# Two-layer hybrid decoder trunk: x normalised before its split, gates leaving PSUM by ScalarE, memory projection first in a layer

## The chip, the cores and the metric

The kernel runs on one core of a Trainium2 chip. The metric is the device time of one execution in microseconds. A core has five engines that run side by side and wait for each other through semaphores: TensorE (PE in the profile, with its weight loads as PEld), VectorE (DVE), ScalarE (ACT), GpSimd (POOL) and SyncE (SP), which here issues the transfers.

## What is computed

Two layers over 1024 tokens of width 1024. Each layer normalises x, projects it by one wide matrix into the inputs of four branches and their gates, runs the branches, and merges them:

```python
h = rms_norm(x, norm_g)
z = h @ w_in          # a_u a_v a_gate b_cq b_ckv b_krope b_gate c_in c_gate m_q m_gate merge_logits
y_a = chunked_spatial_gating(gelu(a_u), gelu(a_v), ...) * silu(a_gate)
y_b = latent_attention(b_cq, b_ckv, b_krope, ...) * silu(b_gate)
y_c = s5_layer(c_in, ...) * silu(c_gate)
y_m = memory_attention(m_q, rms_norm(mem, m_norm_g), ...) * silu(m_gate)
gates = sigmoid(merge_logits + b_merge)
x = x + sum(gates[i] * (y_i @ w_br_i)) @ w_out
```

All of it is float32. TensorE gets each operand as two fp32r parts, hi and lo = value - hi, and forms a product from three matmuls (hi by hi, hi by lo, lo by hi).

## The kernel before, in words

**Tiles.** x is kept transposed: eight chunks of 128 features by 1024 tokens. `make_xg` (L367) multiplies a chunk by `norm_g`, writes its hi part by ACT and its lo part by DVE, and squares it for the norm; the squares are summed over the chunks on GpSimd in `xacc`. The row norm `rs` (one number for each token) is not applied there. Since tokens run along the columns of every product with x, a block of the projection (128 output features by 1024 tokens) can be multiplied by the row norm when it leaves PSUM: `rsb` is the norm of all tokens, copied to every partition, and DVE multiplies each block by it. `x_stats` forms `rs` from `xacc` (16 column sums by TensorE, then a chain of small DVE operations for the inverse square root), and `x_rows` forms `rsb` by four fp32r matmuls.

**A block.** `cm` loads 128 output features' weights (512 KB), splits them (DVE the hi part, mostly GpSimd the lo part, `wsplit` L146), and `block_into` (L184) issues 48 matmuls of 128x128 by 128x512 into a PSUM tile of 1024 columns. There are two such tiles (`pmm`), two smaller for transposes and sums (`ptr`), and two of 512 columns for background work (`pbg`; one in the attention part).

**Order of a layer** (`run`). S5 input (two blocks, `s5_input`), norm, the two blocks of the latent keys and values (`latents`, called ckv below), then the smaller stages of rotary key, memory query, S5 scan (`s5_scan`), keys and values, memory keys and values (`mem_kv`), memory attention, the query latents; in the second part the attention sweep, branch A, the merges (`merge`) and the output projection, whose blocks also prepare the next layer's x. The Tile framework orders each engine's instructions from this program and from priorities. `background` (L1224) is called for 10 of the 32 merge gates and 6 other gate blocks of a layer; their matmuls have the lowest priority and stand wherever TensorE would otherwise wait. Each half (512 tokens) goes to its own `pbg` tile:

```python
for h in range(2):
    with low():
        ps = self.pbg.tile([P, 512], F32, tag="bg", ...)
        self.half_block(ps, (hi, lo), self.xg, hs)
    self.tt(x[:, hs], ps, self.rsb[:, hs], MUL)
```

so the matmuls have the low priority and the multiplication on the way out has the usual one.

**The start.** After the constants, SP loads one S5 input weight, x chunk 0, the second weight and the other chunks. `mem_kv` loads the two raw tiles of the memory itself, splits them, squares them for the memory norm, and projects them with 48 matmuls (four chunks of weights, `m_w_kv`) in the middle of the layer.

Of the kernel before, what the change touches and what calls it, by code (L numbers as in the profile page):

```python
# [8 lines left out]
F32 = mybir.dt.float32  # L9
F32R = mybir.dt.float32r  # L10
# [34 lines left out]
class Trunk:  # L45
    def __init__(self, ctx, tc, a, out, depth):
# [12 lines left out]
        self.nid = 0  # L59
# [86 lines left out]
    def wsplit(self, ap, n, gains=None, keep=False, bg=False, raw=None, eng=None):  # L146

        raw = (self.wraw(bg) if raw is None else raw)[:, :n]
        self.nc.sync.dma_start(out=raw, in_=ap)
# [260 lines left out]
    def x_stats(self):  # L410
        self.rs = self.keep(self.inv_rms(self.tok_sums(self.xacc), 8, D), 8, "rs")

    def x_rows(self):

        hi, lo = self.U("dgh", F32R), self.U("dgl", F32R)
        v = lambda x: x.rearrange("p (t j) -> p t j", t=8)
        wide = lambda x: x.unsqueeze(2).to_broadcast([P, 8, P])
        ident = self.ident.unsqueeze(1).to_broadcast([P, 8, P])
        rh = self.ss(8, "rsh").bitcast(F32R)
        rl = self.ss(8, "rsl")  # L420
        nc = self.nc
        nc.vector.tensor_copy(rh, self.rs)
        self.tt(rl, self.rs, rh.bitcast(F32), SUB)
        self.tt(v(hi), ident, wide(rh.bitcast(F32)), MUL)
        self.tt(v(lo), ident, wide(rl), MUL)
        ps = self.mm()
# [125 lines left out]
    def s5_input(self, l):  # L552

        w = self.wcin if l == 0 else [self.wsplit(self.a["w_cm"][l, B_CIN + b], 1024) for b in range(2)]
# [4 lines left out]
        res = []  # L559
# [87 lines left out]
    def mem_kv(self, l):  # L647
        nc, a = self.nc, self.a
        mh, ml, msum = [], [], []
        mrd = self.U("mrd")  # L650
        for h in range(2):
            raw = self.U("mraw")
            nc.sync.dma_start(out=raw, in_=a["memT"][h])
            hi, lo = self.U("mh", F32R), self.U("ml", F32R)
            self.split(hi, lo, raw)
            sq = self.U("msq")
            self.act(sq, raw, AF.Square)
            rd = mrd[:, h * 256:(h + 1) * 256]
            nc.vector.reduce_sum(out=rd, in_=sq.rearrange("p (b m) -> p m b", b=4), axis=AX.X)
            mh.append(hi)  # L660
            ml.append(lo)
            msum.append(rd)
# [974 lines left out]
```

## Time and profile before

| | |
|---|---|
| median of 3 runs | 2491.41 us (2484.19 to 2493.68) |
| profiled execution | 2490.22 us, its span 2488.5 us |
| mean granted clock of TensorE in it | 0.981 |
| TensorE busy | 2370.0 us, 95% of the span |
| VectorE busy | 1288.2 us, 52% |
| ScalarE busy | 687.4 us, 28% |
| GpSimd busy | 798.1 us, 32% |

The profile is of one execution; the span runs from its first instruction to its last. "Busy" is the time in which an engine had an instruction under way. In a timeline each row is one instruction or a run of alike ones, `out<-in` in the program's names, and in brackets how long the engine had been idle before it and what released it. The granted clock is a share of full speed (2.4 GHz); near 0.5 TensorE is on the lower of its two levels, 1.2 GHz.

### The profile page before, as it was taken

How to read it: one execution, taken by the hardware profiler on the slowest of the kernel's cores; microseconds unless marked ns; L12 is line 12 of the kernel's file. 1: busy time of each engine (PE TensorE's matmuls, PEld its weight loads, DVE VectorE, ACT ScalarE, POOL GpSimd, SP SyncE). 2: the span in 40 equal slices, each digit the busy share in tenths (PEclk: the TensorE clock that was granted, in tenths of full speed). 3: DMA queues.
4: the chain of work that ended last, by engine and by line, in shares of the span. 5: the costliest groups of instructions: out<-in, count | busy, mean ns of one | idle time of the engine just before them, and what ended most of it. 6: DMA issues, size and time to landing. Idle time of an engine off the chain costs nothing. (4 is left out here: it accounts for less than half of the span.)

```text
span 2488.5 us, 28967 instructions
## 1 busy us (share of the span) xinstructions
PE 2370.0 (95%) x11566; PEld 1930.0 (78%) x11566; DVE 1288.2 (52%) x2002; ACT 687.4 (28%) x1110; POOL 798.1 (32%) x616
## 2 busy tenths in 40 slices
PE   7999989989999999999999998999999999999999
PEld 5777677867778887888887876787777788888887
DVE  7554675267776323336335557714688763233351
ACT  3111254136662101111111213622466420011010
POOL 6633112432303214343336431133232132234411
PEclk9989899999999999999999999999999999999999
DMA  3226343242222113123332263413333311112242
GB/s 140 83 75 195 98 148 98 78 126 76 89 70 66 60 34 102 61 92 111 127 95 96 78 186 106 144 45 109 113 90 98 110 50 51 51 60 85 85 166 72
DMA packets 91704, 237.61 MB, mean 95 GB/s; under 512 B 25201, under 2 KB 34353, under 8 KB 91569
## 3 DMA queue, kind: packets, MB, share of 16 engines
q1 hardware_dynamic: 91568, 235.76, 29.7%
q8 instruction: 91, 1.49, 0.3%
q14 instruction: 45, 0.36, 0.0%
HBM read 175.27 MB, written 60.46 MB: 95 GB/s over the span
## 5 line engine op out<-in xcount | busy, mean ns | idle before, releaser
L96 POOL TENSOR_TENSOR wl<-wr,wh 128x1024 fp32r<-128x1024 f32 (+3 forms) x125 | 295.9, 2367 | 998.5 <-DVE wh L152 671.2
L152 DVE CAST wh<-wr 128x1024 fp32r<-128x1024 f32 (+2 forms) x110 | 78.9, 718 | 613.4 <-PE mm L176 542.4
L176 PE MATMUL mm<-xh,wh 128*128 128x512 f32 x1216 | 379.4, 392 | 9.6 <-ACT xh L106 8.3
L176 PE MATMUL mm<-xl,wh 128*128 128x512 f32 x1216 | 376.5, 391 | 0.4 <-DVE xl L103 0.4
L176 PE MATMUL mm<-xh,wl 128*128 128x512 f32 x1216 | 376.1, 390 | 0.2 <-POOL wl L96 0.2
L176 PEld LDWEIGHTS mm<-xh,wh 128*128 128x128 f32 x1216 | 228.0, 189 | 59.5 <-ACT xh L106 8.3
L176 PEld LDWEIGHTS mm<-xl,wh 128*128 128x128 f32 x1216 | 229.3, 189 | 48.8 <-DVE xl L103 0.9
L176 PEld LDWEIGHTS mm<-xh,wl 128*128 128x128 f32 x1216 | 229.1, 188 | 48.4 <-POOL wl L96 0.6
L176 PE MATMUL bg<-xh,bh 128*128 128x512 f32 x576 | 229.8, 416 | 21.6 <-DVE bgx L96 21.6
L176 PE MATMUL bg<-xh,bl 128*128 128x512 f32 x576 | 224.5, 409 | 2.4 <-POOL bl L96 2.4
L176 PE MATMUL bg<-xl,bh 128*128 128x512 f32 x576 | 226.7, 410 | 0.0
L96 POOL TENSOR_TENSOR bl<-br,bh 128x1024 fp32r<-128x1024 f32 x36 | 93.5, 2597 | 305.1 <-DVE bh L152 164.3
L106 ACT ACTIVATE cmn<-cmn,bmh 128x1024 f32<-128x1024 f32 x44 | 50.7, 1151 | 440.0 <-DVE cmn L96 440.0
L176 PE MATMUL pv<-pT,v 128*128 128x256 f32 x640 | 131.4, 307 | 27.3 <-DVE pT L96 21.2
L176 PEld LDWEIGHTS bg<-xh,bh 128*128 128x128 f32 x576 | 111.7, 195 | 48.0 <-DVE bgx L96 28.7
L176 PEld LDWEIGHTS pv<-pT,v 128*128 128x128 f32 x640 | 98.3, 191 | 61.2 <-DVE pT L96 33.1
L96 DVE TENSOR_TENSOR pT<-tr,pT 128x512 fp32r<-128x512 f32 x192 | 129.1, 685 | 30.5 <-ACT pT L106 28.0
L176 PEld LDWEIGHTS bg<-xh,bl 128*128 128x128 f32 x576 | 111.4, 194 | 23.6 <-POOL bl L96 3.2
L106 ACT ACTIVATE pT<-tr 128x512 fp32r<-128x512 f32 x192 | 109.9, 597 | 64.2 <-PE tr L1065 56.0
L176 PEld LDWEIGHTS bg<-xl,bh 128*128 128x128 f32 x576 | 112.1, 195 | 18.6 <-issue 0.2
L1024 DVE TENSOR_REDUCE mx<-mm 128x1 f32<-128x128 f32 (+7 forms) x128 | 96.5, 754 | 36.3 <-PE mm L176 35.6
L106 ACT ACTIVATE pr<-mm,nm,qs 128x128 f32<-128x128 f32 (+7 forms) x128 | 105.9, 832 | 26.3 <-DVE nm L103 26.0
(447 smaller groups left out, 4382.9 us busy)
## 6 DMA issues: line engine op xcount, KB each, us to landing
wr<-in_w_cm_dram SPq DMA_DIRECT2D x76, 512.0 KB, 3.6
br<-in_w_cm_dram SPq DMA_DIRECT2D x36, 512.0 KB, 3.7
bgscr<-bgx SPq DMA_DIRECT2D x20, 512.0 KB, 3.7
gate<-bgscr SPq DMA_DIRECT2D x20, 512.0 KB, 5.4
ysscr<-bgx SPq DMA_DIRECT2D x16, 512.0 KB, 2.6
br<-ysscr SPq DMA_DIRECT2D x16, 512.0 KB, 3.5
wr<-in_w_out_dram SPq DMA_DIRECT2D x16, 512.0 KB, 3.9
bgr<-riscr SPq DMA_DIRECT2D x24, 256.0 KB, 5.4
```

Source lines behind the costliest of these rows:

```text
L96: (eng or self.nc.vector).tensor_tensor(out=out, in0=x, in1=y, op=op)
L106: self.nc.scalar.activation(out, x, f, **k)
L152: self.nc.vector.tensor_copy(hi[:, :n], raw)
L176: self.nc.tensor.matmul(out, lhsT, rhs, start=start, stop=stop)
L1024: nc.vector.reduce_max(out=mx, in_=ps[:, 0:n], axis=AX.X)
```

## The change

- **x is normalised before its split.** `make_xg` now comes after `x_stats`, and multiplies each chunk in place by `norm_g` and `rsb` (eight DVE operations for a layer) before ACT and DVE split it. No block is multiplied by `rsb` on its way out any more. `rsb` comes from two fp32 matmuls in place of four fp32r ones; `x_rows` and `s5_spread` go. The squares (`x_square`) are ACT's, the sums DVE's in layer 0, GpSimd's in layer 1 except the last.
- **Gates leave PSUM by ACT.** The tanh of a gate reads PSUM itself; plain blocks are copied by ACT. In `background` the whole body has the low priority. The S5 input goes straight to `ct` by an ACT copy.
- **Memory first.** `mem_load` and `mem_project` stand at the start of the program for layer 0, and in the output projection of layer 0 (blocks 4 and 7) for layer 1; ACT copies the projection to `mkv`, which `mem_kv`, now right behind ckv, reads. SP loads two memory tiles and two of their weights ahead of x, and no S5 weight early.
- **38 buffers** of 4 KB for each partition in the general pool, 35 before, and a dynamic DMA scratch of 1024.

```diff
 def wsplit(...)
-        self.nc.sync.dma_start(out=raw, in_=ap)
+        if ap is not None:
+            self.nc.sync.dma_start(out=raw, in_=ap)
...
-    def make_xg(self, l, c, xt):
-        hi, lo = self.U(f"xh{c}", F32R), self.U(f"xl{c}", F32R)
-        self.split(hi, lo, xt, gain=self.norm_g[:, l * 8 + c:l * 8 + c + 1])
+    def x_square(self, c, xt, eng):
         if c == 0:
             self.xacc = self.wraw(True)
-            self.xg = []
-            if l == 0:
-                self.tt(self.xacc, xt, xt, MUL, eng=self.nc.gpsimd)
-            else:
-                self.act(self.xacc, xt, AF.Square)
+            self.act(self.xacc, xt, AF.Square)
         else:
             sq = self.U("xsq")
             self.act(sq, xt, AF.Square)
-            self.tt(self.xacc, self.xacc, sq, ADD, eng=self.nc.gpsimd)
-        self.xg.append((hi, lo))
+            self.tt(self.xacc, self.xacc, sq, ADD, eng=eng)
+
+    def make_xg(self, l, xs):
+        self.xg = []
+        for c, xt in enumerate(xs):
+            hi, lo = self.U(f"xh{c}", F32R), self.U(f"xl{c}", F32R)
+            self.stt(xt, xt, self.norm_g[:, l * 8 + c:l * 8 + c + 1], self.rsb, MUL, MUL)
+            self.split(hi, lo, xt)
+            self.xg.append((hi, lo))
...
     def x_stats(self):
-        self.rs = self.keep(self.inv_rms(self.tok_sums(self.xacc), 8, D), 8, "rs")
-    def x_rows(self):
...
-            self.mmr(ps[:, hs], self.onesr, hi[:, hs], True, False)
-            self.mmr(ps[:, hs], self.onesr, lo[:, hs], False, True)
-        self.rsb = self.U("rsb")
-        self.act(self.rsb, ps, AF.Copy)
+        rs = self.inv_rms(self.tok_sums(self.xacc), 8, D)
+        dg = self.U("dg")
+        self.tt(dg.rearrange("p (t j) -> p t j", t=8), self.ident.unsqueeze(1).to_broadcast([P, 8, P]),
+                rs.unsqueeze(2).to_broadcast([P, 8, P]), MUL)
+        self.rsb = self.U("rsb")
+        for h in range(2):
+            hs = slice(h * 512, (h + 1) * 512)
+            ps = self.tr()
+            self.nc.tensor.matmul(ps, self.onesr.bitcast(F32), dg[:, hs], start=True, stop=True)
+            self.act(self.rsb[:, hs], ps, AF.Copy)
...
     def s5_input(self, l):
-        w = self.wcin if l == 0 else [self.wsplit(self.a["w_cm"][l, B_CIN + b], 1024) for b in range(2)]
+        w = [self.wsplit(self.a["w_cm"][l, B_CIN + b], 1024) for b in range(2)]
...
-            cr = self.U("cr")
-            self.act(cr, ps[b], AF.Copy)
-            res.append(cr)
-        return res
-    def s5_spread(self, cin):
-        for b, cr in enumerate(cin):
             ct = self.U("ct")
-            self.tt(ct.rearrange("p (s j) -> p j s", s=8), cr.rearrange("p (j s) -> p j s", s=8),
-                    self.rsb.rearrange("p (j s) -> p j s", s=8), MUL)
+            self.act(ct.rearrange("p (s j) -> p j s", s=8), ps[b].rearrange("p (j s) -> p j s", s=8), AF.Copy)
...
-    def mem_kv(self, l):
+    def mem_load(self, l):
+        raws = [self.U("mraw") for _ in range(2)]
+        for h in range(2):
+            self.nc.sync.dma_start(out=raws[h], in_=self.a["memT"][h])
+        self.mem, mrd = [], self.U("mrd")
...
+    def mem_project(self, l):
+        nc, a = self.nc, self.a
+        mh, ml, msum = [[m[k] for m in self.mem] for k in range(3)]
+        self.rsm = self.keep(self.inv_rms(self.tok_sums(msum[0], 2), 2, D), 2, "rsm")
         ps = self.mm()
...
+        self.mkv = self.U("mkv")
+        self.act(self.mkv, ps, AF.Copy)
+
+    def mem_kv(self, l):
+        nc, rsm = self.nc, self.rsm
+        pv = self.mkv.rearrange("p (t w) -> p t w", t=2)
...
     def cmn(self, l, bi):
         t = self.U("cmn")
-        self.tt(t, self.cm(l, bi, self.xg), self.rsb, MUL)
+        self.act(t, self.cm(l, bi, self.xg), AF.Copy)
...
     def background(...):
         x = ft("bgx")
-        for h in range(2):
-            hs = slice(h * 512, (h + 1) * 512)
-            with low():
+        sg = ft("bgs") if y is not None else x
+        with low():
+            for h in range(2):
+                hs = slice(h * 512, (h + 1) * 512)
                 ps = self.pbg.tile([P, 512], F32, tag="bg", name=self._n("bg"))
                 self.half_block(ps, (hi, lo), self.xg, hs)
-            self.tt(x[:, hs], ps, self.rsb[:, hs], MUL)
-        with low():
+                self.act(sg[:, hs], ps, AF.Tanh, scale=0.5, **({} if bias is None else {"bias": bias}))
+                if y is not None:
+                    self.stt(x[:, hs], sg[:, hs], 1.0, ps, ADD, MUL)
             if y is None:
-                self.act(x, x, AF.Tanh, scale=0.5, bias=bias)
                 nc.sync.dma_start(out=dst, in_=x)
                 return
-            sg = ft("bgs")
-            self.act(sg, x, AF.Tanh, scale=0.5)
-            self.stt(x, sg, 1.0, x, ADD, MUL)
...
     def merge(...):
-                g = self.cmn(l, B_MRG + 8 * i + c)
-                self.act(g, g, AF.Tanh, scale=0.5, bias=self.bm_half[:, l * 32 + 8 * i + c:l * 32 + 8 * i + c + 1])
+                g = self.U("gate")
+                self.act(g, self.cm(l, B_MRG + 8 * i + c, self.xg), AF.Tanh, scale=0.5, bias=self.bm_half[:, l * 32 + 8 * i + c:l * 32 + 8 * i + c + 1])
...
     def run(self):
-        self.wcin = [self.wsplit(a["w_cm"][0, B_CIN], 1024, eng=nc.vector)]
+        self.mwr = [self.wraw() for _ in range(2)]
+        self.mem_load(0)
+        for c in range(2):
+            nc.sync.dma_start(out=self.mwr[c], in_=a["m_w_kv"][0, c])
         xs = [self.U("x") for _ in range(8)]
         for c in range(8):
             nc.sync.dma_start(out=xs[c], in_=a["xT"][c])
...
+        self.setup()
+        self.mem_project(0)
         for c in range(8):
-            self.make_xg(0, c, xs[c])
-        self.setup()
+            self.x_square(c, xs[c], nc.vector)
...
-            cin = self.s5_input(l)
             self.x_stats()
+            self.make_xg(l, xs)
+            self.s5_input(l)
...
-            self.ckv, kacc = self.latents(l, B_CKV, 2, "kv", self.gkv_norm, ((self.x_rows, lambda: self.s5_spread(cin)),))
+            self.ckv, kacc = self.latents(l, B_CKV, 2, "kv", self.gkv_norm)
+            self.mem_kv(l)
...
             scan(1)
-            self.mem_kv(l)
             glu()
...
                 if l < self.L - 1:
-                    self.make_xg(l + 1, c, xr)
+                    if c == 7:
+                        self.mem_project(l + 1)
+                    self.x_square(c, xr, nc.vector if c == 7 else nc.gpsimd)
+                    xs[c] = xr
+                    if c == 4:
+                        self.mwr = []
+                        self.mem_load(l + 1)
...
-NU = 35
+NU = 38
```

Where the instructions stand. **ACT, start of layer 0, after.** `wh` are weights of the memory projection, `mkv` its copy out of PSUM, `br` and `xsq` the squares of x:

```order
L106 ACTIVATE br_282<-x_116 128x1024
L106 ACTIVATE wh_242<-wr_240,consts_90 128x512 x2
L106 ACTIVATE wh_262<-wr_260,consts_90 128x512 x2
L106 ACTIVATE mkv_280<-mm_203 128x1024
L106 ACTIVATE xsq_284<-x_117 128x1024
L106 ACTIVATE xsq_287<-x_118 128x1024
```

Five more squares follow. The copy `mkv` stands between the first square and the other seven. Before, these squares alternate with the hi parts, and no `mkv` is there.

**ACT, end of layer 0's output projection, after.** `xres` are the output blocks, the last being `xres_9338`:

```order
L106 ACTIVATE xsq_9335<-xres_9276 128x1024
L106 ACTIVATE wh_9442<-wr_9440,consts_90 128x512 x2
L106 ACTIVATE wh_9462<-wr_9460,consts_90 128x512 x2
L106 ACTIVATE wh_9482<-wr_9480,consts_90 128x512 x2
L106 ACTIVATE mkv_9500<-mm_9419 128x1024
L106 ACTIVATE xsq_9502<-xres_9338 128x1024
L106 ACTIVATE rsb_9538<-tr_9539 128x512
L106 ACTIVATE rsb_9538<-tr_9542 128x512
L106 ACTIVATE xh_1622_9545<-xres_8885 128x1024
```

Here `mkv` stands ahead of the square of the last block only; the others are through.

**PE, background blocks, before** (layer 0, behind ckv; `bg_614` and `bg_640` are the halves of one block, `bh` and `bl` its weights):

```order
L176 MATMUL bg_640<-xh_20_126,bl_610 128x512
L176 MATMUL bg_614<-xh_23_133,bh_609 128x512
L176 MATMUL bg_640<-xh_23_133,bh_609 128x512
L176 MATMUL bg_614<-xl_24_134,bh_609 128x512
L176 MATMUL bg_640<-xl_24_134,bh_609 128x512
L176 MATMUL bg_614<-xh_23_133,bl_610 128x512
L176 MATMUL bg_640<-xh_23_133,bl_610 128x512
L176 MATMUL bg_614<-xh_26_140,bh_609 128x512
```

**PE, background blocks, after** (layer 0, a later place; `bg_1023` and `bg_1049` are the halves of one block):

```order
L177 MATMUL bg_1023<-xh_79_373,bl_1019 128x512
L177 MATMUL bg_1023<-xh_81_378,bh_1018 128x512
L177 MATMUL bg_1023<-xl_82_379,bh_1018 128x512
L177 MATMUL bg_1023<-xh_81_378,bl_1019 128x512
L177 MATMUL bg_1049<-xh_67_343,bh_1018 128x512
L177 MATMUL bg_1049<-xl_68_344,bh_1018 128x512
L177 MATMUL bg_1049<-xh_67_343,bl_1019 128x512
L177 MATMUL bg_1049<-xh_69_348,bh_1018 128x512
```

The halves took turns before; now the second begins when the first has ended.

## Rows read from the trace of the kernel before

**Rows 1.** The page, busy time of TensorE.

```profile
PE 2370.0 (95%) x11566; PEld 1930.0 (78%) x11566; DVE 1288.2 (52%) x2002; ACT 687.4 (28%) x1110; POOL 798.1 (32%) x616
```

**Rows 2.** PE's waits (total, times, longest): whole run; 60 to 500 us; 1320 to 1640 us.

```profile
PE bg L176 <- DVE bgx L96: 21.6, 15, 3.9
...
PE bg L176 <- DVE bgx L96: 12.5, 7, 3.9
...
PE tr L500 <- DVE stt L96: 5.3, 1, 5.3
PE bg L176 <- DVE bgx L96: 5.1, 4, 2.7
```

**Rows 3.** Windows by stage: length, busy of PE, PEld, DVE, ACT, POOL; clock, DMA, GB/s.

```profile
240.00:300.00 60.00, 50.59 (x214) 38.60 (x213) 37.19 (x73) 8.52 (x11) 9.35 (x5) 0.83 0.35 109
...
1640.00:1720.00 80.00, 80.00 (x353) 64.44 (x352) 22.98 (x22) 15.20 (x15) 30.06 (x14) 1.00 0.25 80
```

**Rows 4.** Narrow windows, the same columns.

```profile
38.00:46.00 8.00, 7.86 (x29) 6.85 (x30) 5.93 (x23) 0.00 (x0) 5.99 (x4) 0.57 0.30 82
...
260.00:281.00 21.00, 21.00 (x62) 15.75 (x61) 7.84 (x14) 2.00 (x2) 0.00 (x0) 0.51 0.18 51
...
1741.00:1752.00 11.00, 7.11 (x18) 5.26 (x19) 10.45 (x29) 2.01 (x2) 4.72 (x2) 0.53 0.67 211
```

**Rows 5.** Timeline of PE, 0 to 75 us: start, us, instruction, idle before and releaser.

```profile
8.27 1.22 PE L176 MATMUL mm<-xh,wh 128*128 128x512 f32 x2 [8.27 <-ACT xh L106]
...
38.15 3.27 PE L388 MATMUL tr<-ones,br 128*128 128x1 f32 x16 [3.99 <-POOL br L96]
...
73.08 0.61 PE L176 MATMUL mm<-xh,wl 128*128 128x512 f32 x2
```

**Rows 6.** Timeline of PE, 258.5 to 259.5 us.

```profile
258.81 0.71 PE L620 MATMUL tr<-sx,cst 64*128 64x127 f32 x4 [2.88 <-DVE sx L96]
259.44 0.50 PE L176 MATMUL bg<-xh,bh 128*128 128x512 f32 x1
```

**Rows 7.** Timeline of DVE, 0 to 10 us.

```profile
5.71 0.69 DVE L152 CAST wh<-wr 128x1024 fp32r<-128x1024 f32 x1 [2.29 <-DMA wr<-in_w_cm_dram]
...
8.27 1.70 DVE L152 CAST wh<-wr 128x1024 fp32r<-128x1024 f32 x1 [0.60 <-DMA wr<-in_w_cm_dram]
```

**Rows 8.** Groups of DVE by form: times, busy us, mean ns; idle before and releasers.

```profile
L96 DVE TENSOR_TENSOR bgx<-bg,rsb 128x512 f32<-128x512 f32 x72 | 47.4, 684 | 43.2 <-PE bg L176 42.9
...
L103 DVE SCALAR_TENSOR_TENSOR xl<-x,consts,xh 128x1024 fp32r<-128x1024 f32 x8 | 20.4, 2623 | 0.0
...
L103 DVE SCALAR_TENSOR_TENSOR wl<-wr,consts,wh 128x512 fp32r<-128x512 f32 x16 | 12.7, 807 | 3.8 <-ACT wh L106 3.8
...
L103 DVE SCALAR_TENSOR_TENSOR xl<-xres,consts,xh 128x1024 fp32r<-128x1024 f32 x8 | 10.4, 1296 | 10.0 <-ACT xh L106 10.0
...
L96 DVE TENSOR_TENSOR ml<-mraw,mh 128x1024 fp32r<-128x1024 f32 x4 | 4.9, 1222 | 1.2 <-ACT mh L106 1.2
```

**Rows 9.** Timeline of ACT, 30 to 36 us.

```profile
32.84 1.03 ACT L106 ACTIVATE cr<-mm 128x1024 f32<-128x1024 f32 x1 [9.08 <-PE mm L176]
```

**Rows 10.** Timeline of DVE, the memory norm, 290 to 294 us.

```profile
290.64 0.16 DVE L100 TENSOR_SCALAR ms<-tr 128x2 f32<-128x2 f32 x1 [0.42 <-PE tr L388]
...
293.66 0.17 DVE L407 COPY rsm<-ry 128x2 f32<-128x2 f32 x1
```

**Rows 11.** Groups of PE by form, 0 to 73.6 us.

```profile
L176 PE MATMUL bg<-xh,bh 128*128 128x512 f32 x4 | 2.0, 512 | 0.0
...
L176 PE MATMUL mm<-dgh,onesr 128*128 128x512 f32 x2 | 1.1, 550 | 3.2 <-DVE s5w L96 3.2
```

**Rows 12.** Line 516, the fp32 matmuls (records: ns min/median/max).

```profile
L516 PE MATMUL tr<-sd,shift x64: 270/275/275, 98.6 to 1417.3; 128*128 128x128 f32 x64
```

**Rows 13.** Groups of ACT by form.

```profile
L106 ACT ACTIVATE pT<-tr 128x512 fp32r<-128x512 f32 x192 | 109.9, 597 | 64.2 <-PE tr L1065 56.0 <-PE tr L1139 6.7
```

**Rows 14.** Timeline of POOL, 15 to 36 us.

```profile
15.86 19.18 POOL L96 TENSOR_TENSOR br<-br,xsq 128x1024 f32<-128x1024 f32 x6
```

More of the change, by code (lines that the diff above doesn't have):

```diff
@@ L58, in __init__ @@
         self.dp = mk(name="dp", bufs=1, space=bass.MemoryType.DRAM)
-        self.nid = 0
+        self.nid, self.ppv = 0, None
     def _n(self, base):
@@ L644, in s5_glu @@
             nc.sync.dma_start(out=self.gscr[b], in_=sg)
-    def mem_kv(self, l):
-        nc, a = self.nc, self.a
-        mh, ml, msum = [], [], []
-        mrd = self.U("mrd")
-        for h in range(2):
[L652 to L662, printed above, removed]
-        self.tt(msum[0], msum[0], msum[1], ADD)
-        rsm = self.keep(self.inv_rms(self.tok_sums(msum[0], 2), 2, D), 2, "rsm")
+    def mem_load(self, l):
[4 more added lines that the diff above has]
+        for h in range(2):
+            hi, lo = self.U("mh", F32R), self.U("ml", F32R)
+            self.split(hi, lo, raws[h])
+            sq = self.U("msq")
+            self.act(sq, raws[h], AF.Square)
+            rd = mrd[:, h * 256:(h + 1) * 256]
+            self.nc.vector.reduce_sum(out=rd, in_=sq.rearrange("p (b m) -> p m b", b=4), axis=AX.X)
+            self.mem.append((hi, lo, rd))
+        self.tt(mrd[:, 0:256], mrd[:, 0:256], mrd[:, 256:512], ADD)
+    def mem_project(self, l):
+        nc, a = self.nc, self.a
+        mh, ml, msum = [[m[k] for m in self.mem] for k in range(3)]
+        self.rsm = self.keep(self.inv_rms(self.tok_sums(msum[0], 2), 2, D), 2, "rsm")
         ps = self.mm()
@@ L667, in mem_kv @@
             gains = [self.gm_norm[:, l * 8 + 2 * c + k:l * 8 + 2 * c + k + 1] for k in range(2)]
-            wh, wl = self.wsplit(a["m_w_kv"][l, c], 1024, gains)
+            wh, wl = self.wsplit(None if c < len(self.mwr) else a["m_w_kv"][l, c], 1024, gains,
+                                 raw=self.mwr[c] if c < len(self.mwr) else None)
             for k in range(2):
@@ L675, in mem_kv @@
                                  wa[:, k * 512:(k + 1) * 512], kt == 0 and j == 0, kt == 7 and j == 2)
-        pv = ps.rearrange("p (t w) -> p t w", t=2)
+        self.mkv = self.U("mkv")
[3 more added lines that the diff above has]
+        pv = self.mkv.rearrange("p (t w) -> p t w", t=2)
         sq = self.U("ksq")
@@ L727, in mq_stage @@
             nc.vector.tensor_copy(ssm.rearrange("p (t h) -> p t h", t=8)[:, :, 2 * p:2 * p + 2], self.head_sums(sqs[p], self.sel2, 2))
-        pre = self.ss(32, "pre")
-        nc.vector.tensor_copy(pre.rearrange("p (t h) -> p t h", t=8), self.rs.unsqueeze(2).to_broadcast([P, 8, 4]))
-        r = self.inv_rms(ssm, 32, 64, pre)
+        r = self.inv_rms(ssm, 32, 64)
         self.mqs = self.lp.tile([P, 32], F32, tag="mqs", name=self._n("mqs"))
@@ L754, in krope @@
         kc, kr = self.U("kc"), self.U("kr")
-        self.tt(kc[0:64, :], ps[0:64, :], self.rsb[0:64, :], MUL)
+        self.act(kc[0:64, :], ps[0:64, :], AF.Copy)
         pt = self.tr()
@@ L804, in rope_query_tables, with latents @@
         return res
-    def latents(self, l, first, n, base, gain, between=()):
+    def latents(self, l, first, n, base, gain):
         res = []
@@ L811, in latents @@
             ps = self.cm(l, first + b, self.xg)
-            if b < len(between):
-                for f in between[b]:
-                    f()
             hi, lo = self.U(f"{base}h{b}", F32R), self.U(f"{base}l{b}", F32R)
@@ L887, in q_stage @@
         pv = pt[:, 0:80].rearrange("p (t m) -> p m t", t=8)
-        alq = self.inv_rms(pv[:, 8], 8, 768, self.rs)
+        alq = self.inv_rms(pv[:, 8], 8, 768)
         pre, ssq = self.ss(64, "pre"), self.ss(64, "ssq")
@@ L1282, in silu2 @@
     def silu2(self, l, bi):
-        x = self.cmn(l, bi)
+        x = self.cm(l, bi, self.xg)
         sg = self.U("sg")
@@ L1319, in branch_a @@
             v, tmp = self.U("av"), self.U("avt")
-            self.tt(v.rearrange("p (t c) -> p t c", t=4), ps.rearrange("p (t c) -> p t c", t=4),
-                    self.rs[:, 4 * tg:4 * tg + 4].unsqueeze(2).to_broadcast([P, 4, 256]), MUL)
+            self.act(v, ps, AF.Copy)
             self.gelu2(v, v, tmp)
@@ L1455, in run @@
             self.mq_stage(l)
-            self.bkv = self.keep(self.inv_rms(self.tok_sums(kacc), 8, 256, self.rs), 8, "bkv")
+            self.bkv = self.keep(self.inv_rms(self.tok_sums(kacc), 8, 256), 8, "bkv")
             def scan(q):
@@ L1625 @@
     arrs = _layout(inputs)
-    nc = bacc.Bacc("TRN2", target_bir_lowering=False, num_devices=1)
+    nc = bacc.Bacc("TRN2", target_bir_lowering=False, num_devices=1, dynamic_dma_scratch_size=1024)
     arrays, aps = {}, {}
```

16 lines of the change are left out of this document (removed).

## The prediction, on record before the changed kernel's time was known

> **What bounds the kernel now.** I read the page's totals first, then PE's waits, the windows by stage, and the timelines of the start. TensorE (PE) is busy for 2370.0 us of the 2488.5 us span [rows 1], so the kernel is long because PE has that much to multiply; only 118 us are idle. The change leaves the count of large matmuls alone. It can gain or lose in two places only: PE's idle gaps, and the stretches after a gap in which the granted clock is low. The largest group of gaps is the background blocks waiting for VectorE (DVE) to empty their PSUM bank, 21.6 us in 15 waits [rows 2]. The stretches show that not every gap matters alike: 1640 to 1720 us is full at clock 1.00, while 240 to 300 us has 50.59 us of work in 60 at a mean clock of 0.83 [rows 3]. Inside the latter PE is never idle from 260 to 281 us, yet it runs at 0.51, the lower of the clock's two levels, behind a gap of 2.88 us at 258.81; 38 to 46 us (0.57) follows one of 3.99 us, and 1741 to 1752 us (0.53) has 3.9 us of idle time in it [rows 4 to 6].
>
> **1. The start of layer 0.** Today PE begins the S5 input blocks at 8.27 us, as soon as one chunk of x has landed, and needs no row norm for that; the norm is applied when results leave PSUM. Its chain runs beside the matmuls and shows as a wait of 3.99 us at 38.15; both ckv blocks are done at 73.5 [rows 5]. After the change nothing that reads x can start before the norm is known. What PE has instead is the memory projection (48 matmuls), which needs weights of its own. Loads follow each other by 1.28 us: between DVE's first and second weight casts, at 5.71 and 8.27, three transfers of 512 KB end, two intervals [rows 7]. On SP's queue now stand two raw memory tiles, two weights, eight chunks of x, then two more weights whose buffers must first come free. The fourth weight is the fourteenth such load and lands at 5.7 + 13 x 1.28 = 22.3. Its hi and lo copies take about 0.8 each by halves [rows 8], and its 12 matmuls 0.45 apiece at the low clock, to which PE falls while it waits for weights: 24.0 + 5.4 = about **30**. Moving x two loads back costs nothing, since its squares are not needed before that.
>
> For ScalarE (ACT) stands in order: the copy mkv, which needs the projection's last matmul, is listed ahead of seven of the eight squares. So the norm's chain begins at 30: mkv and the first square 1.0 each, as the pass `cr` of the same size [rows 9]; seven DVE adds at 1.22, priced by the subtraction ml of equal shape [rows 8], 8.6; 16 column sums 3.3 [rows 5]; the rsqrt chain, 290.64 to 293.83 where the memory norm has it now, 3.2 [rows 10]; the diagonal, a DVE pass of the same size, 1.2; two fp32 matmuls and a copy out; the product with x 1.3, as xl with xres [rows 8], and its hi copy 1.1. The trace has no fp32 matmul of 512 columns. Below, it costs what the fp32r one does, 0.55 [rows 11]; above, the fp32 matmul of 128 columns, two records of 0.275 for each, scales to 2.2 [rows 12]. I take 1.7 each, near the upper end, because the fp32 row is the same number format, and 0.6 for the copy, as for pT, 128x512 out of PSUM [rows 13]: 4.0. Sum: 30 + 1.0 + 9.6 + 3.3 + 3.2 + 1.2 + 4.0 + 2.4 = **54.7**. From there 96 matmuls of the S5 input and 96 of ckv at 0.227 (353 in the full 80 us from 1640 to 1720 [rows 3]) take 43.6, plus 3.4 because the clock starts low (8 us at 0.57 [rows 4]): 101.7 against 73.5, 28.2 later. By then PE has 48 matmuls (10.9) done that it now does later, and lacks the 12 background matmuls that it now fits in (2.7) [rows 11]. Net **+20**; +13 if the chain is shorter at each unknown price, +25 if the port below makes it longer.
>
> Here a page speaks against the change too. That ACT's instruction waits in line is what today's row shows: ACT does nothing for 9.08 us ahead of `cr`, until PE's block ends [rows 9]. The Trainium skill (TensorE: Matmul & The Clock Gate, Architectural detail) calls the queues of ScalarE and VectorE strict FIFO. By it the squares wait for mkv, and the sum below is as it stands; without it they would run as the chunks land, and up to 10.6 us (1.0 + 9.6) of this loss, and of the sum, would go.
>
> **2. The layer boundary.** Call E the end of the last out-projection block. Today the next layer's input blocks follow at once. In the change the second memory projection does (10.9, and 11.5 with the sums of its own norm; its raw tiles are loaded three blocks ahead and its weights under the blocks, hidden, 5 if not), then again mkv ahead of the last square: 11.5 + 1.0 + 1.0 + 1.2 for the one add left + 3.3 + 3.2 + 1.2 + 4.0 + 2.4 = 28.8 after E. Of that PE spends 10.9 on work that leaves another place, and 3.8 on what it does today as well (the sums, at half of 3.3 on the other level of the clock, and four row matmuls of 0.55). Idle: 14.1; with a low clock afterwards, some 3: **+17** (12 to 20).
>
> **3. The exits.** 72 background halves leave by DVE today at 0.684 each, full blocks likewise, and 16 multiplications of x (1.3) come in [rows 8]; DVE gets lighter, which by itself is worth nothing, since PE waits for single results and not for DVE's total. What counts is the order. Before, both halves of a block alternate on PE, so both banks close within one matmul and the next block must wait for an eviction; after, most halves run one after the other, so a bank has up to 24 matmuls' time (5.4 us) to be emptied (of the 28 halves that layer 0 runs ahead of its attention, eight still alternate, second halves of neighbouring blocks). ACT then needs about 0.6 for it [rows 13]. Of the 21.6 us I credit: 60 to 500 us, 12.5 of bank waits [rows 2] and half of the 2.9 before sx [rows 6], less some 3 that stay (those eight halves; a tanh queued behind Sin and squares on ACT): -11. Layer 1: bank waits 5.1 and the wait of 5.3 for DVE's stt [rows 2], less 2.4 that stay: -8. Attention: the rest of the bank waits, 4.0, nearly all: -4. Together **-23**. In these bounds, all stays (0) or all goes (-28).
>
> **4. The clock behind those gaps.** 260 to 281 loses 10.3 us by its 0.51 (21 x 0.49), 1741 to 1752 5.2, 38 to 46 3.4 [rows 4], and a few like the last lie elsewhere; together some 20. If the gaps shrink, so may these; some only move. I take -13, two thirds, between 5 and 20: the memory projection that runs just there today goes to the start.
>
> **5. Nothing else.** The remaining stages are full at 1.00 [rows 3]. Three more buffers and the smaller scratch name no wait in the trace: 0.
>
> Sum: 20 + 17 - 23 - 13 = **+1** on the profiled execution, 2490.2, which stands 1.2 below the median of 2491.4. Forecast **2492 us**, no change. A measurement of this kernel can tell some 0.5% (12 us) from none.
>
> **Rivals.** *Faster, about 2469*: the middle gives back all (-28 and -20), and the start and the boundary cost 13 and 12: -23. For it: the gaps and low stretches are plain. Against: both new chains are counted step by step.
> *Slower, about 2514*: the scan stages (240 to 300, 1480 to 1560) are bound by DVE's and ACT's own chains, and background matmuls only fill them. Then a gap taken from a bank shows up as one before the scan, the low clock with it, and the middle returns only about 15: 20 + 17 - 15 = +22. It decides where filler runs out before the scan's results come. For: at 258.81 PE waited for sx, and background matmuls stood behind that [rows 6]. Against: 21.6 us of waits are for a bank alone [rows 2].
> *Slower, about 2508*: today x's eight subtractions take 2.6 each while GpSimd adds beside them, and 1.3 in layer 1 [rows 8, 14]. So DVE keeps half its pace while a GpSimd operation runs, 3.2 each there (six in 19.18). In the change DVE does 16 two-input operations per layer with PE behind them; if the GpSimd subtractions of the two S5 input, two ckv and one background weights fall among them, that is 2 layers x 5 x 1.6 = +16. The Trainium skill (SBUF — State Buffer, SBUF: two separate sides) gives GpSimd and such DVE operations one port pair, held by one at a time; the 2.6 beside 1.3 agrees. Against: the weights' subtractions are mostly done before the norm is.
> *It does nothing* at the exits (banks wait for ACT as they did for DVE): +37 - 5 for the clock, 2523.
>
> **How the numbers follow.** Forecast 0.38, faster 0.30, scan-bound 0.19, port 0.09, nothing at the exits 0.04. So faster 0.30, same 0.38, slower 0.32. The range 2464 to 2518 reaches to just beyond the first two rivals, for their own spread; the forecast's own is 2480 to 2504.
>
> **What would show it.** PE's first x matmul (S5 input) at about 55 us instead of 8, and a gap of some 20 us before it, released by the hi copy; a second gap of 12 to 15 us at about 1290; PE's bank waits below 7 us in total; 260 to 281 back near full clock. If the S5 input starts before 45, or the boundary gap is below 8, the faster rival holds; if bank waits are gone and waits for sx, su or the scan have grown as much, the scan-bound one.

## The result, and the profile after

The changed kernel takes **2586.9 us** (median of 4 runs, 2580.1 to 2592.8) against 2489.4 before: ratio 1.0392, 95% interval 1.0357 to 1.0426. That is some 97 us slower, and far outside the range. The profiled execution spans 2587.3 us. On its page TensorE's row, which answers to [rows 1]:

```profile
PE 2405.8 (93%) x11566; PEld 1952.7 (75%) x11566; DVE 1137.8 (44%) x1879; ACT 710.5 (27%) x1163; POOL 766.6 (30%) x608
```

PE is idle for 181.5 us instead of 118.5 (span less busy time): +63.0. It is busy for 2405.8 instead of 2370.0 with the same number of matmuls, because more of them ran on the low clock (mean 0.961 instead of 0.981): +35.8. Together these are the difference of the spans.

Windows by stage, cut at the same places of the program in both kernels (first matmul of the first scan, of the second, first of the attention sweep, end of its values, end of layer 0; columns as in [rows 3]). Before:

```profile
0.00:144.60 144.60, 123.40 (x534) 99.04 (x534) 85.42 (x212) 35.09 (x42) 83.36 (x111) 0.92 0.33 113
144.60:243.90 99.30, 92.67 (x492) 75.92 (x491) 54.47 (x113) 21.35 (x26) 38.16 (x78) 0.98 0.45 129
243.90:530.80 286.90, 267.94 (x1211) 211.32 (x1212) 156.70 (x218) 95.86 (x164) 70.22 (x31) 0.96 0.34 108
530.80:750.00 219.20, 198.27 (x1209) 160.16 (x1208) 170.23 (x305) 133.68 (x265) 54.06 (x27) 0.98 0.28 87
750.00:1262.40 512.40, 510.46 (x2340) 423.53 (x2339) 201.07 (x209) 77.34 (x80) 177.08 (x78) 1.00 0.26 85
1262.40:1384.00 121.60, 116.08 (x540) 93.79 (x538) 57.47 (x114) 16.29 (x18) 55.87 (x86) 0.94 0.27 86
1384.00:1482.30 98.30, 93.11 (x492) 75.95 (x491) 55.60 (x118) 20.91 (x26) 38.83 (x78) 0.98 0.46 128
1482.30:1738.10 255.80, 242.25 (x1143) 192.00 (x1143) 135.71 (x199) 89.06 (x158) 65.83 (x30) 0.99 0.33 106
1738.10:1974.00 235.90, 217.04 (x1289) 175.78 (x1287) 182.84 (x318) 137.14 (x269) 56.76 (x28) 0.97 0.31 94
1974.00:2488.50 514.50, 508.78 (x2334) 422.54 (x2333) 188.73 (x201) 60.72 (x64) 157.89 (x71) 1.00 0.25 82
```

After:

```profile
0.00:174.10 174.10, 136.97 (x602) 107.06 (x602) 103.13 (x283) 54.36 (x68) 59.42 (x105) 0.92 0.32 107
174.10:272.20 98.10, 78.57 (x431) 64.64 (x430) 40.81 (x76) 17.07 (x23) 35.76 (x78) 0.93 0.42 119
272.20:522.00 249.80, 239.22 (x1074) 187.29 (x1075) 112.45 (x146) 86.81 (x154) 64.71 (x28) 0.95 0.31 99
522.00:780.00 258.00, 228.24 (x1326) 184.46 (x1324) 177.24 (x311) 136.65 (x274) 61.19 (x29) 0.97 0.30 94
780.00:1298.90 518.90, 513.27 (x2354) 426.40 (x2353) 158.96 (x181) 78.69 (x84) 169.31 (x77) 1.00 0.26 84
1298.90:1453.50 154.60, 138.06 (x609) 109.07 (x607) 72.64 (x186) 37.42 (x44) 58.15 (x88) 0.90 0.28 90
1453.50:1561.90 108.40, 89.06 (x429) 72.62 (x428) 41.01 (x76) 17.08 (x23) 35.56 (x78) 0.83 0.35 96
1561.90:1796.30 234.40, 227.84 (x1036) 179.46 (x1037) 100.14 (x136) 78.33 (x146) 63.39 (x27) 0.95 0.30 99
1796.30:2062.00 265.70, 238.50 (x1364) 193.41 (x1362) 179.83 (x312) 138.04 (x276) 62.26 (x30) 0.96 0.29 92
2062.00:2587.30 525.30, 516.06 (x2358) 428.25 (x2356) 151.59 (x176) 66.00 (x71) 156.82 (x71) 1.00 0.25 81
```

Length less PE's busy time is the idle time of a stage; the clock's column tells the rest:

| stage | idle before, after (layer 0) | clock | idle before, after (layer 1) | clock |
|---|---|---|---|---|
| to the first scan | 21.2, 37.1 | 0.92, 0.92 | 5.5, 16.5 | 0.94, 0.90 |
| first to second scan | 6.6, 19.5 | 0.98, 0.93 | 5.2, 19.3 | 0.98, 0.83 |
| second scan to attention | 19.0, 10.6 | 0.96, 0.95 | 13.6, 6.6 | 0.99, 0.95 |
| attention sweep | 20.9, 29.8 | 0.98, 0.97 | 18.9, 27.2 | 0.97, 0.96 |
| merges, output | 1.9, 5.6 | 1.00, 1.00 | 5.7, 9.2 | 1.00, 1.00 |

The first line is what the prediction counted for the start and the boundary. The second is new: between the scans PE runs 431 matmuls instead of 492 in layer 0, and idles more and at a lower clock (part of that low clock falls into the new gap itself, 0.65 from 257 to 272 us, where PE has nothing to slow down). The stage is not longer in layer 0 (98.1 us for 99.3): what it lost is the work that filled it. The fourth has more matmuls (1326 instead of 1209, 1364 instead of 1289): background work that used to be done earlier.

PE's waits in the changed kernel, answering to [rows 2] (total, times, longest):

```profile
PE mm L571 <- DMA su<-cscr: 29.4, 2, 14.8
...
PE bg L177 <- DVE bgx L103: 13.3, 6, 3.9
...
PE mm L177 <- ACT gate L106: 6.4, 2, 3.2
...
PE bg L177 <- ACT bgx L106: 5.2, 5, 3.5
```

The waits for a bank fell only from 21.6 to 18.5 (13.3 + 5.2), and 29.4 us of waits for `su`, the scan's input, stand beside them (3.6 before). By place the bank waits went two ways. Ahead of the attention sweep they fell from 18.0 to 5.2. In the sweep, where background work has one bank, they rose from 3.6 to 13.3. The two sweeps (layers 0 and 1) before, then after:

```profile
PE bg L176 <- DVE bgx L96: 0.2, 1, 0.2
PE bg L176 <- DVE bgx L96: 3.4, 2, 3.1
...
PE bg L177 <- DVE bgx L103: 5.3, 2, 3.9
PE bg L177 <- DVE bgx L103: 8.0, 4, 3.9
```

There a gate with a product now leaves its bank by two passes, both at the lowest priority. In the longest wait of layer 0 ACT takes the tanh at 567.18; DVE multiplies at 570.25, behind a cast of weights that it could begin only at 568.32, when they had landed; PE goes on at 571.00, after 3.85 us.

PE's timeline at the first wait for `su`, and the windows around it (`sx` is a later tile of the scan):

```profile
256.37 1.03 PE L961 MATMUL tr<-ident,kro 128*128 128x128 f32 x8
272.19 3.35 PE L571 MATMUL mm<-su,wst 128*64 128x128 f32 x32 [14.79 <-DMA su<-cscr]
...
287.32 0.71 PE L603 MATMUL tr<-sx,cst 64*128 64x127 f32 x4 [2.03 <-DVE sx L96]
```

```profile
257.00:272.00 15.00, 0.40 (x4) 0.16 (x2) 0.00 (x0) 1.23 (x3) 0.00 (x0) 0.65 0.85 269
272.00:289.00 17.00, 14.40 (x79) 11.22 (x80) 13.43 (x22) 1.04 (x2) 4.76 (x2) 0.90 0.54 195
289.00:309.00 20.00, 20.00 (x58) 15.00 (x58) 6.06 (x12) 3.08 (x4) 0.00 (x0) 0.50 0.11 31
```

PE does nothing for 14.79 us, nor do DVE and POOL; only the transfers run, at 269 GB/s. The 20 us at 0.50 do not follow right behind the gap (272 to 289 us is at 0.90) but behind the wait for `sx` at 287.32, the place of the second scan at which the kernel before has its low stretch from 260 to 281. Why PE has no work is seen on SP, which issues the transfers one after the other (`br`: raw weights of a background block; `bh`, `bl`: their hi and lo parts; start, us):

```profile
182.95 0.33 SPq L150 DMA_DIRECT2D br<-in_w_cm_dram  x1
...
256.54 2.04 SPq L963 DMA_DIRECT2D kscr<-krt  x2
...
265.70 1.00 SPq L563 DMA_DIRECT2D su<-cscr  x1
266.80 1.11 SPq L150 DMA_DIRECT2D br<-in_w_cm_dram  x1
```

DVE and GpSimd take the weights out of `br`:

```profile
241.68 0.69 DVE L153 CAST bh<-br 128x1024 fp32r<-128x1024 f32 x1 [1.77 <-PE bg L177]
...
242.51 2.35 POOL L96 TENSOR_TENSOR bl<-br,bh 128x1024 fp32r<-128x1024 f32 x1 [18.08 <-PE bg L177]
```

From 182.95 to 266.80 no background weights are asked for. There is one raw buffer, and until 244.86 it holds the weights asked for at 182.95: they are cast only when PE has done with an earlier block, whose matmuls rest from 212.24 to 234.64 while PE has other work. From 244.86 on the next load stands in the queue behind the keys' transfers, which wait for ACT, and behind `su`. By then PE had used up the blocks it had; its last background matmul starts at 256.13. For `su` itself SP shows no wait but its turn in this queue; no run issued it ahead of the keys' transfers.

### The profile page after: what moved, and what is told of

It is laid out like the page before. It is cut to its first block, busy times and chain, and to the rows that moved or that the text cites. A ratio compares the mean times of both kernels' runs of the same rounds, so it can differ in the third digit from the quotient of the medians.

```text
span 2587.3 us, 28869 instructions
## 1 busy us (share of the span) xinstructions
PE 2405.8 (93%) x11566; PEld 1952.7 (75%) x11566; DVE 1137.8 (44%) x1879; ACT 710.5 (27%) x1163; POOL 766.6 (30%) x608
## 4 chain that ended last, share of the span: by engine, by line
PE 76%; DVE 11%; DMA 5%; ACT 3%; POOL 2%; issue 2%; SPq 1%; DVEq 0%; ACTq 0%; POOLq 0%
PE mm L177 55%; PE bg L177 9%; PE pv L177 3%; PE tr L177 2%; PE tr L1053 2%; DMA br<-in_w_cm_dram 2%; DVE nm L103 1%; POOL bl L96 1%; DVE mx L1012 1%; DVE pT L96 1%; PE tr L819 1%; DVE bh L153 1%; PE tr L603 1%; DVE bgx L103 1%; DMA br<-ysscr 1%
## 5 line engine op out<-in xcount | busy, mean ns | idle before, releaser
L177 PE MATMUL bg<-xh,bh 128*128 128x512 f32 x576 | 238.1, 423 | 18.5 <-DVE bgx L103 13.3
L177 PE MATMUL bg<-xh,bl 128*128 128x512 f32 x576 | 235.0, 418 | 5.4 <-POOL bl L96 3.3
L177 PE MATMUL bg<-xl,bh 128*128 128x512 f32 x576 | 234.6, 416 | 0.0
L106 ACT ACTIVATE gate<-mm,bmh 128x1024 f32<-128x1024 f32 x44 | 49.1, 1117 | 482.0 <-PE mm L177 482.0
L177 PEld LDWEIGHTS bg<-xh,bh 128*128 128x128 f32 x576 | 114.6, 199 | 46.4 <-DVE bgx L103 16.5
L177 PEld LDWEIGHTS bg<-xl,bh 128*128 128x128 f32 x576 | 114.2, 199 | 20.9 <-issue 0.9
```

The costliest lines, as they stand in the source:

```text
L106: self.nc.scalar.activation(out, x, f, **k)
L177: self.nc.tensor.matmul(out, lhsT, rhs, start=start, stop=stop)
```

## The experiments

An exit is what takes a background half out of its PSUM bank. All medians in us; "ratio" is to the kernel before, run on the same chip beside it. PE's busy and idle time are of the profiled execution, which lies up to 13 us from the median.

| run | median | ratio (95% interval) | PE busy | idle |
|---|---|---|---|---|
| e1 exits by ACT, usual priority | 2535.4 | 1.0190 (1.0159 to 1.0221) | 2385.0 | 141.0 |
| e2 exits by DVE, usual priority | 2556.3 | 1.0279 (1.0248 to 1.0309) | 2402.5 | 157.7 |
| e3 memory in the middle | 2583.2 | 1.0374 (1.0340 to 1.0408) | 2393.2 | 175.7 |
| e4 = e2 + e3 | 2514.3 | 1.0101 (1.0068 to 1.0133) | 2378.3 | 144.1 |
| e5 = e1 + e3 | 2542.1 | 1.0223 (1.0180 to 1.0265) | 2403.5 | 150.2 |
| e6 = e1, norm chain first | 2523.6 | 1.0142 (1.0119 to 1.0165) | 2389.2 | 133.6 |
| e7 before, exits at low priority | 2514.9 | 1.0116 (1.0081 to 1.0152) | 2395.9 | 130.0 |
| e8 = e5, merge gates out by DVE | 2541.7 | 1.0208 (1.0173 to 1.0244) | 2394.9 | 147.3 |
| e9 change, two raw weight buffers | 2539.5 | 1.0206 (1.0176 to 1.0237) | 2391.5 | 154.3 |
| e10 before, two raw weight buffers | 2476.9 | 0.9957 (0.9937 to 0.9976) | 2376.6 | 105.0 |
| e11 = e6, two raw weight buffers | 2499.8 | 1.0032 (1.0008 to 1.0055) | 2381.6 | 118.9 |
| e12 = e4, two raw weight buffers | 2503.0 | 1.0037 (1.0015 to 1.0058) | 2357.3 | 137.6 |

The diff had put a background block's way out of PSUM under the lowest priority, with its matmuls. Theory A is that this lost the time; B that the memory projection had been the filler between the scans; C that ACT is a poor exit.

**e1: exits at the usual priority.**

```diff
-        with low():
-            for h in range(2):
-                hs = ...
+        for h in range(2):
+            hs = ...
+            with low():
                 ps = self.pbg.tile([P, 512], F32, tag="bg", ...)
                 self.half_block(ps, (hi, lo), self.xg, hs)
-                self.act(sg[:, hs], ps, AF.Tanh, ...)
+            self.act(sg[:, hs], ps, AF.Tanh, ...)
...
```

> The changed kernel, with one thing put back: the background blocks' way out of PSUM (tanh by ACT, product by DVE) at the usual priority, the matmuls alone at the lowest. Theory A (the exits at lowest priority let less background work be done ahead of the attention; 65 more of layer 0's matmuls now stand ahead of it, 49 more of layer 1's): about half of the 61 us that the middle and the attention lost come back, 2555 to 2565 us; the wait for su (29.4 us) shrinks, low clock between the two scans too. Theory B (what lost the time is that the memory projection no longer fills the gap between the scans, whatever the exits do): no change within 8 us, 2579 to 2595, waits for su stay near 29. Theory C (ACT as the exit is itself too slow or too full): no change or slower.

2535.4: 51.5 below the changed kernel, more than A had asked. The waits for `su` are nearly gone, and SP asks for one more block's weights ahead of the keys' transfers (at 212.67):

```profile
PE mm L571 <- DMA su<-cscr: 4.7, 2, 2.8
```

```profile
174.88 0.33 SPq L150 DMA_DIRECT2D br<-in_w_cm_dram  x1
...
212.67 0.33 SPq L150 DMA_DIRECT2D br<-in_w_cm_dram  x1
...
260.04 1.90 SPq L963 DMA_DIRECT2D kscr<-krt  x2
```

**e2: exits by DVE**, a copy at the usual priority, then one tanh of the block.

```diff
...
+            self.nc.vector.tensor_copy(x[:, hs], ps)
...
+                self.act(x, x, AF.Tanh, scale=0.5, bias=bias)
...
```

> The changed kernel with background blocks leaving PSUM as before: a DVE copy of each half (where before multiplied) at the usual priority, then one tanh of the whole block by ACT at the lowest. 618 instead of 511 background matmuls of layer 0 stand ahead of the attention (641 before). Theory A: most of what the middle and attention lost returns, 2530 to 2550 us. Theory B: 2575 to 2595. Theory C (ACT): as A, and clearly (over 10 us) below the run with ACT exits at the usual priority.

2556.3: 30.6 back, less than A had asked, and 21 us worse than e1. C falls here: with the memory first, ACT at the usual priority is the better exit. PE's bank waits are 19.8 us in 18 times, with e1 13.0 (6.8 for DVE, 6.2 for ACT).

**e3: memory in the middle**, exits as changed.

```diff
-        self.mem_project(0)
...
             scan(1)
+            self.mwr = []
+            self.mem_load(l)
+            self.mem_project(l)
+            self.mem_kv(l)
             glu()
...
```

> The changed kernel with the memory projection back in the middle of the layer (loads, norm, projection and keys behind the second scan, as before), all else as changed. Theory B: the waits for su fall below 8 us in total and the low clock between the scans with them, 30 to 45 us back there; the start and the boundary now have no matmuls to run beside the norm chain, but the chain starts up to 18 us (layer 0) and 12 us (layer 1) earlier: total 2535 to 2560 us. Theory A: the waits for su stay above 20 us and the time is within 12 us of the changed kernel's.

2583.2, 3.7 below the changed kernel; the waits for `su` stay at 20.4 us. B alone falls.

**e4: both of the last.**

> Both of the last two: memory projection in the middle, background out by DVE. What then remains of the change is x normalised before its split, ACT copies of plain blocks and gates of the merges, and the buffers. Background matmuls stand ahead of the attention in the same number as before (641 and 572). If A and B together hold the whole loss beside the start: 2489 plus what the norm ahead of the split costs at the start and boundary, 15 to 35 us: 2505 to 2525. If the ACT copies or buffers cost anything: above 2530.

2514.3: 42 below e2, where e3 gave 4. So with these exits the memory's place costs, where with the exits as changed it did not. What is left, 28 us (ratio 1.0101), is the normalisation ahead of the split, the ACT copies and the buffers, which this run does not tell apart.

**e5: e1 and e3 together.**

> Exits by ACT at the usual priority (as the first run) and the memory projection in the middle (as the third). If the memory projection's place costs by itself, as the step from the second run to the fourth says (42 us with exits by DVE), this is 25 to 40 us below the first run: 2495 to 2512 us, with no wait for su over 5 us. If its place only matters when background work runs short, it stays within 12 us of the first run's 2535. If ACT exits are worth more than DVE's (bank waits 7 us in the first run, 20 in the second), it is below the fourth run's 2514.

2542.1: within 12 us of e1, as the second theory has it (the place matters only when background work runs short; PE waits 2.4 us for `su`), but 28 above e4, which none of them has: with the memory in the middle DVE is the better exit. In the profiled executions PE is idle only 6 us longer than in e4 but busy 25 us longer, so most of that loss is in low-clock stretches (mean clock 0.966, in e4 0.976). Why they come in this order of instructions and not in e4's stays open.

**e6: e1 with the norm chain first.**

```diff
-        self.mem_project(0)
...
             self.x_stats()
+            self.mem_project(l)
             self.make_xg(l, xs)
...
-                    if c == 7:
-                        self.mem_project(l + 1)
```

> The first run (exits by ACT at the usual priority, memory first), with the squares and the norm of x ahead of the memory projection in the program, so that ACT squares before it copies mkv, and PE forms the column sums between the projection's matmuls. If the norm chain standing behind mkv is what the start and boundary cost (the gap of 14.2 us before the column sums in layer 0, 3.8 in layer 1, and what follows): 18 to 25 us below the first run, 2510 to 2518. If x's loads or the weights of the projection set the start: within 8 us of 2535.

2523.6: 11.8 below e1, about half of what was expected. The squares now run as the chunks land, and the S5 input begins at 44.23 instead of 56.09 (timelines of ACT and PE in e6):

```profile
13.55 3.02 ACT L106 ACTIVATE xsq<-x 128x1024 f32<-128x1024 f32 x3
...
20.64 1.06 ACT L106 ACTIVATE xsq<-x 128x1024 f32<-128x1024 f32 x1 [0.21 <-DMA x<-in_xT_dram]
...
34.94 1.02 ACT L106 ACTIVATE mkv<-mm 128x1024 f32<-128x1024 f32 x1
```

```profile
44.23 1.65 PE L177 MATMUL mm<-xh,wh 128*128 128x512 f32 x3 [8.53 <-ACT xh L106]
```

**e7: the kernel before, its exit at the lowest priority.**

```diff
                 self.half_block(ps, (hi, lo), self.xg, hs)
-            self.tt(x[:, hs], ps, self.rsb[:, hs], MUL)
+                self.tt(x[:, hs], ps, self.rsb[:, hs], MUL)
```

> The kernel before, with one thing changed: the DVE multiplication that empties a background bank gets the lowest priority like its matmuls. 612 instead of 641 background matmuls of layer 0 then stand ahead of the attention, 551 instead of 572 in layer 1. If the priority of the exit alone loses time, whichever engine does it: 2495 to 2515 us, the attention 5 to 12 us longer. If it needs the move to ACT: within 6 us of before.

2514.9, at the upper end of what was expected: 27 above before, from an indentation. So the priority costs by itself and with DVE too. In the profiled execution, which lies 12.7 above the median, 11.5 us are idle time and 25.9 PE's longer busy time. It is not the gap of the changed kernel: PE has no wait for `su`, and waits 20.1 us for banks instead of 21.6. Which waits cost it here stays open.

**e8: e5 with merge gates out by DVE.**

```diff
-                self.act(g, self.cm(...), AF.Tanh, ...)
+                nc.vector.tensor_copy(g, self.cm(...))
+                self.act(g, g, AF.Tanh, ...)
```

> The fifth kernel of these (ACT exits at the usual priority, memory in the middle) with the merge gates copied out of PSUM by DVE and the tanh taken in place by ACT, as before. The merges and output projections lost 4 to 7 us per layer in every run with ACT exits, with waits of PE for ACT's gate of 3 to 4 us: if that is the cause, 6 to 12 us below the fifth; if it is the other ACT copies or the background spilled into the merges, within 4 us of it.

2541.7, the same as e5. The waits for ACT's gates went (the merges idle for 1.9 and 6.5 us instead of 4.9 and 9.4), but the total does not show the 6 us; with intervals of some 10 us to either side it could not rule them out.

**e9: the change with two raw buffers** for background weights (`br`), 35 general buffers.

```diff
-            return self.bp.tile([P, 1024], F32, tag="br", bufs=1, ...)
+            return self.bp.tile([P, 1024], F32, tag="br", bufs=2, ...)
-NU = 38
+NU = 35
```

> The changed kernel, exits still at the lowest priority, with two raw buffers for background weights instead of one (35 general buffers instead of 38 to make room). 336 background matmuls of layer 0 then stand ahead of the second scan instead of 240, so two more blocks are fed before SP's queue stands still behind the key stage's stores. If running out of background work there is what makes the gaps of 14.8 and 14.6 us before su and the low clock around them: those gaps fall below 4 us and the kernel comes to 2535 to 2555 us. If the exits cost time in another way: gaps filled but the time lost elsewhere, 2570 to 2590.

2539.5, within what was expected if the shortage makes the gap: 47.4 back with the exits left at the lowest priority. Two loads more go out ahead of the keys' transfers, PE no longer waits for `su`, and between the scans the clock is 0.97 and 1.00 instead of 0.93 and 0.83:

```profile
249.47 1.74 SPq L150 DMA_DIRECT2D br<-in_w_cm_dram  x2
...
267.58 1.90 SPq L963 DMA_DIRECT2D kscr<-krt  x2
```

```profile
180.10:287.30 107.20, 101.44 (x518) 81.86 (x517) 40.11 (x79) 18.45 (x25) 40.15 (x80) 0.97 0.45 133
1442.10:1547.70 105.60, 98.35 (x518) 79.61 (x517) 40.10 (x79) 18.46 (x25) 40.34 (x80) 1.00 0.42 123
```

Two remedies that touch different things, e1 the exits and e9 the supply, each fill the same gap. That settles what the gap is: background work runs out there. It does not settle the whole loss. Both stay some 50 us above the kernel before, with the start and the boundary much as changed, and in e9, its exits still at the lowest priority, the bank waits of the attention stay too (16.0 us; 4.3 in e1).

**e10: the kernel before with two raw buffers** (and the small DMA scratch).

> The kernel before with two raw buffers for background weights (and the small DMA scratch of the change to make room). 311 instead of 288 background matmuls ahead of the second scan, 647 instead of 641 ahead of the attention. If background work is short there before too: 2470 to 2483 us. If it is not, within 6 us of before.

2476.9, ratio 0.9957 (0.9937 to 0.9976): 12 us below the kernel before and faster than both, within what was expected. Its waits for `su` (3.6 us) are gone, but its bank waits fell by more, from 21.6 to 14.2, so a shortage at the same place is only a part of it.

**e11 and e12: e6 and e4 with two raw buffers.**

> The sixth kernel (exits by ACT at the usual priority, norm chain ahead of the memory projection) with two raw buffers for background weights, 35 general ones. If more background work ahead of the attention helps (599 instead of 576): 2505 to 2518 us; if the rest of its loss is the start, the boundary and the clock: within 6 us of 2523.6.

> The fourth kernel (exits by DVE at the usual priority, memory projection in the middle) with two raw buffers for background weights, 35 general ones: what is left of the change is the normalisation ahead of the split and the ACT copies of plain blocks and merge gates. If the buffers matter, 2495 to 2508 us; if not, within 6 us of 2514. Below before (2488) only if the normalisation's cost at the start and boundary, 24 us, is made up elsewhere.

2499.8 (more than expected) and 2503.0: 23.8 and 11.3 back. With these remedies together the change stands 0.3 to 0.4% above before; against e10, which has the same buffers, 23 and 26 us.

## Why the prediction was wrong, step by step

**Step 1, the start: right, one term by luck.** The S5 input began at 56.09 us (forecast 54.7), after gaps of 14.15, 3.82 and 3.10. The chain in the changed kernel, on PE and ACT:

```profile
41.85 3.57 PE L391 MATMUL tr<-ones,br 128*128 128x1 f32 x16 [14.15 <-DVE br L96]
49.25 3.75 PE L423 MATMUL tr<-dg,onesr 128*128 128x512 f32 x4 [3.82 <-DVE dg L96]
56.09 1.67 PE L177 MATMUL mm<-xh,wh 128*128 128x512 f32 x4 [3.10 <-ACT xh L106]
```

```profile
27.74 1.02 ACT L106 ACTIVATE mkv<-mm 128x1024 f32<-128x1024 f32 x1 [3.98 <-PE mm L177]
28.66 6.72 ACT L106 ACTIVATE xsq<-x 128x1024 f32<-128x1024 f32 x7
```

The copy mkv stands ahead of the seven squares, as the listing said, at 27.74 instead of 30. Two fp32 matmuls took 3.75 us (1.7 each forecast), but on the low clock, where the sum had not put them; in e6, at clock 1.00, both take 1.98. That this term came out is luck. Idle to the first scan grew by 15.9 us, with the clock by some 18 (net +20 forecast). What ACT's order is worth shows in e6: with mkv behind the squares they run from 13.55 as the chunks land, not at 28.66 behind mkv, and the input began 11.9 us earlier (10.6 was the bound). This agrees with the strict FIFO that the Trainium skill (TensorE: Matmul & The Clock Gate, Architectural detail) gives that queue. In the profiled executions e6 reaches the first scan 14.3 us ahead of e1, and the second 8.0 ahead.

**Step 2, the boundary: right in the sum.** 11.0 us more idle (14.1 forecast) and a clock of 0.90 instead of 0.94: 0.10 x 154.6 - 0.06 x 121.6 = 8 (3 forecast), about +19 for +17.

**Step 3, the exits: wrong, and this is the step that failed.** It put -23 on "What counts is the order": halves one behind the other, so that banks are empty in time. Ahead of the attention that came true, 12.8 us less of bank waits, as did the shorter wait for `stt` (2.1 us for 6.2). But in the attention, where "nearly all" of 4.0 was to go, bank waits grew by 9.7: with one bank no half can start before the last has left it, in whatever order they run. And ahead of the second scans 25.8 us of new waits for `su` took the place of what was gained. The text had the exits' new priority before it in the diff, and costed the tanh by its 0.6 us and not by when it gets its turn. More, it counted gaps and never asked how much background work lies ready where PE has nothing else. It put 28 background halves ahead of layer 0's attention, as many as the program calls there; in PE's order 511 matmuls stand there, some 21 halves (641 matmuls before, of 864 in a layer: ten merge gates and eight other gates, where the text on the kernel before has six). Between the scans PE lives on the blocks fed before the raw buffer and then SP's queue hold up the next; the change fed one block fewer (in the order of PE's instructions 240 background matmuls instead of 288 stand ahead of the second scan) and had taken the memory projection, 48 matmuls, from behind it. What the runs showed in place of the -23 is 14.8 and 14.6 us of gap, and 117 and 75 matmuls pushed into the attention, where idle time grew by 8.9 and 8.3 (5.1 and 4.6 of it bank waits).

**Step 4, the clock: wrong too.** -13 was forecast; PE's busy time grew by 35.8. The stretch 260 to 281 did not go: it is the one from 289 to 309, at the same place of the second scan, behind a wait for `sx` of 2.03 us instead of 2.88. It stands in e1 and e9 too, without the gap (0.50 from 290 to 313 and from 297 to 320). New low stretches came in layer 1, whose clock from the first scan to the attention was 0.98 and 0.99 and is now 0.83 and 0.95.

**Step 5: nearly right.** 0 was forecast; the merges lost 3.7 and 3.5 us, partly to waits for ACT's gates. That taking these waits away shortens the kernel is not shown (e8).

**The rivals.** The scan-bound one named the place and the point ("where filler runs out before the scan's results come") and the sign that would show it, waits for su: ahead of the attention bank waits went and waits for su came. But it let the middle still give back 15, when it lost some 55 (98.8 less 18 at the start, 19 at the boundary, 7 in the merges): it was priced as a gain foregone, not as a new gap. GpSimd's port was not put to the test: x's products took 1.28 each and the subtractions 1.22, but GpSimd stood idle beside all but the last of them (52.2 to 71.97 us in layer 0). That 35 or 38 buffers matter was not tried alone.

## What to carry to other kernels

Before crediting a shorter wait at a filler, count how much filler is ready at each place where the engine has nothing else, and what its supply waits for: here one raw buffer, and then a place in the DMA queue. The instruction that frees a buffer belongs to the priority of whoever waits for the buffer, not to that of the work it ends; moving it cost 27 to 51 us in three pairs of kernels (e1, e5 against e3, e7), in e7 without longer bank waits. And when a block of matmuls is moved to fill one hole, look for the hole it filled before.

## What was not expected of the hardware

The same gap can be followed by either clock. In the changed kernel PE waits 2.62 us for `sx` in both layers, at 187.07 and 1466.43, with the same program. The 20 us that follow:

```profile
187.00:207.00 20.00, 19.93 (x117) 16.35 (x118) 10.14 (x22) 3.63 (x6) 8.76 (x15) 1.00 0.17 53
1466.40:1486.40 20.00, 19.96 (x59) 15.04 (x60) 10.43 (x21) 0.69 (x1) 2.11 (x2) 0.50 0.00 0
```

117 matmuls at clock 1.00 the first time, 59 at 0.50 the second. So the clock's part of a change, here 36 of 97 us, can't be read off the gaps alone.

Nor do parts add. Moving the memory projection to the middle was worth 42 us with DVE exits at the usual priority, and nothing clear with exits at the lowest (4 less) or with ACT exits (7 more); each such step also rearranges where the low stretches fall.
